# First block's attention: value products of two heads emitted in turn, and the low parts of the keys kept on both halves of the partitions

## The chip, the cores and the metric

The kernel runs on one core of one Trainium2 chip. The metric is the time on the device of one execution, in microseconds (us); a run is repeated, and the median stands. A core has five engines that work beside each other: PE (TensorE, matrix products and, as PEld, the loads of their weights), DVE (VectorE), ACT (ScalarE), POOL (GpSimd) and SP (SyncE, which starts transfers here). PE writes its products to PSUM, from where DVE and ACT fetch them.

## The reference

Two blocks follow each other, each of two layers, on 256 tokens of width 1024 and 256 context tokens. The change lies in the attention of the first block, which is, for one layer:

```python
h  = modulate(rms_norm(x,  norm_mix[l]), sh1, sc1)
hc = modulate(rms_norm(xc, norm_mix[l]), csh1, csc1)
k, v, q, u, f, gt = jnp.split(h @ w_in[l], IN_SPLITS, axis=-1)
kc, vc, qc, uc, fc, gtc = jnp.split(hc @ w_in[l], IN_SPLITS, axis=-1)   # layer 0
q = apply_rope(q.reshape(B, T, N_Q_HEADS, HEAD_DIM), cos, sin)
k = apply_rope(k.reshape(B, T, N_KV_HEADS, HEAD_DIM), cos, sin)
o = latent_attention(q, k, v, kc, vc, attn_sink[l])
x = x + g1 * merge_branches(o, u, f, gt, ...)
oc = context_attention(qc, kc, vc, attn_sink[l])                        # layer 0 only
```

There are 8 query heads on 2 key/value heads, of 64 channels each. A latent query sees the 256 latent keys, under a window of 128 to either side, the 256 context keys, and one sink column in the softmax. A context query (layer 0 only) sees the context keys and the sink. `latent_attention` is products q k, mask, softmax, and products of the probabilities p with v. The same layer holds a pooling branch, a Fourier branch, 24 gate tiles and a merge, then a feed-forward part with a convolution. The second block holds stick-breaking attention, an mLSTM, a spatial gating and a feed-forward part that gathers 128 experts for each token. All is computed in float32.

## The kernel before

The whole is one program, and a scheduler sets the order of the instructions on each engine; PE then runs in that order. Activations lie with channels on the 128 partitions and tokens along the free dimension.

Dense products (`fm`, `mm3`, lines 165 to 182) split both operands into a high and a low part and add three products for each block of 128 channels: high by high (L169), low by high (L170), high by low (L171). One such product has 512 columns in layer 0 (latents and context) and 256 in layer 1 (latents only). In the trace such operands are named `b`, `hi` and `lo`, and their PSUM tiles `mm`.

In `layer1` the query tile `ot` (passed on as `qt`) holds, for head m + 4·kv, the high part of the query on the partitions of kv (0 to 63 for kv 0, 64 to 127 for kv 1) and the low part on the other 64. `keys()` (lines 489 to 504) fills `kt` with three slots of 512: slot kv holds the high part of kv's keys on both halves, slot 2 the low part of kv 0's keys on the lower 64 partitions and of kv 1's on the upper 64. `tt` (L117) is a two-tensor operation on DVE. `kt` and the values `vu` appear as `s` in the trace, query tiles as `b`.

In `attention` each head is a generator with three stages:

1. scores: one product of 128 partitions with slot kv (both parts of the query by the high part of the keys), one of 64 with slot 2 (high part of the query by the low part of the keys), for latents one masking product with `k_mask`; then maximum and bias on DVE and the exponential on ACT.
2. the probabilities are transposed in blocks of 128 (L138, a product with the identity `k_sq`) and copied from PSUM (`ptb`, in the trace `t`), by ACT for odd heads, by DVE for even ones.
3. value products: for each block of 128 keys one product of 64 channels into `ob`, an `sm` tile of PSUM in which kv 0 owns partitions 0 to 63 and kv 1 the others. There are four blocks for a latent head, two for a context head. In the trace they are `sm<-t,s 128*64`, two records for a product.

All bank products, scores and values alike, pass through `Bank.mm`, so they carry the line 45. For each m, heads are gone through in the order i = 0, 1, 2, ..., with kv = i mod 2; a step of the loop calls stage 3 of head i-2, stage 2 of head i-1 and stage 1 of head i, and then one of the `fill` functions (a gate tile of 24 dense products, a pooling or a Fourier part). Layer 0 has 32 heads (16 latent, 16 context), layer 1 has 16, all latent. `mod_step` (L264 in layer 0) spreads a product with the modulation weights through the program: four of its products share one bank on different strips of it.

`ptb` and the other 512-wide tiles come from a pool of five buffers (`t2`); the `sm` tiles of PSUM from a pool of four banks.

Of the kernel before, what the change touches and what calls it, by code (L numbers as in the profile page):

```python
# [10 lines left out]
F32 = mybir.dt.float32  # L11
F32R = mybir.dt.float32r
# [4 lines left out]
OP = mybir.AluOpType  # L17
AX = mybir.AxisListType

P = 128  # L20
# [9 lines left out]
HALVES = ((slice(0, 64), 0), (slice(64, 128), 1))  # L30
# [36 lines left out]
class Kernel:  # L67
# [375 lines left out]
    def layer1(self, l, x):  # L443
# [8 lines left out]
        def rope(out, src):  # L452
            raw = self.t2([P, 512])[:, :T]
            self.copy(raw, src)
            rot = self.psum("sm")[:, :T]
            nc.tensor.matmul(rot, rotm, raw, start=True, stop=True)
            a = self.t2([P, 512])[:, :T]
            b = self.t2([P, 512])[:, :T]
            self.tt(a, raw, cosT, OP.mult)
            self.tt(b, rot, sinT, OP.mult)  # L460
            self.tt(out, a, b, OP.add)

        vk = self.s8([P, 2048])
        ff = self.s8([P, 2, 512])
        kt = self.s8([P, 3, 512], F32R)
        vu = vk[:, :1536].rearrange("p (b c) -> p b c", b=4)
        banks = [self.psum("sm") for _ in range(2 if last else 4)]
        for u in range(4):
# [5 lines left out]
            for tb, bank in enumerate(banks):  # L474
                for kk in range(2):
                    k = 2 * u + kk
# [12 lines left out]
        def keys():  # L489
            ps = self.fm(self.unit(d["w_in"][l, 0]), h, 0, KD, 0, 512)  # L490
            k = self.t2([P, 512])
            rope(k[:, :T], ps[:, :T])
            self.copy(k[:, T:], ps[:, T:])
            for r, i in HALVES:
                self.copy(kt[r, i], k[r])
                self.copy(kt[HALVES[1 - i][0], i], k[r])
                self.tt(kt[r, 2], k[r], kt[r, i].bitcast(F32), OP.subtract)
            if last:
                vt = self.t2([P, 512])[:, :T]
                self.copy(vt, self.fm(self.unit(d["w_in"][l, 31]), h, 0, KD, T, 512))  # L500
                ps = self.psum("sm")
                for tb in range(2):
                    self.transpose(ps[:, tb * P:(tb + 1) * P], vt[:, tb * P:(tb + 1) * P])
                self.copy(vu[:, 2:, :P], ps[:, :T].rearrange("p (b c) -> p b c", b=2))

        if not last:
            keys()
# [19 lines left out]
        if last:  # L527
            keys()
# [27 lines left out]
        for m in range(KD):  # L556
            w = self.unit(d["w_br"][l, m])
            acc = None
            for b, src, wk0, nk in ((1, po, 4, 2), (2, fo, 6, 2), (0, o, 0, 4)):
# [3 lines left out]
                if acc is not None:  # L563
                    s = self.t2([P, 512])[:, :n]
# [21 lines left out]
    def attention(self, l, kt, qt, vu, o, n):  # L586

        nc = self.nc  # L590
        nsink = self.sb([P, 8], "ns")
        self.ts(nsink, self.sink[:, l], -1.0, None, OP.mult)
        nq = n // P

        def head(m, i, blk):
            qb, kv = divmod(i, 2)
            lat = qb < 2
            k0, nk = (0, 512) if lat else (T, T)
            nb = nk // P
            if i == 0:  # L600
                blk.update(ob=Bank(self, "sm"), nm=self.sb([P, 8], "c1"), den=self.sb([P, 8], "c1"))
            ob, nm, den = blk["ob"], blk["nm"], blk["den"]
            hh = kv * 4 + m
            r = slice(kv * 64, kv * 64 + 64)
            qs = slice(qb * P, (qb + 1) * P)
            bank = Bank(self, "sm")
            s = bank.t[:, :nk]
            bank.mm(s, qt[:, m + 4 * kv, qs], kt[:, kv, k0:k0 + nk])
            bank.mm(s, qt[r, m + 4 * kv, qs], kt[r, 2, k0:k0 + nk])
            if lat:  # L610
                b = 1 - qb
                bank.mm(s[:, b * P:(b + 1) * P], *((self.le_neg, self.ident16) if qb else (self.ident16, self.le_neg)))
            mx = self.sb([P, 1], "m1")
            nc.vector.tensor_reduce(mx, s, axis=AX.X, op=OP.max)
            self.ts(nm[:, i:i + 1], mx, -0.125, nsink[:, hh:hh + 1], OP.mult, OP.min)
            p = self.t2([P, 512])[:, :nk]
            self.act(p, s, AF.Exp, scale=0.125, bias=nm[:, i:i + 1], accum_out=den[:, i:i + 1])
            yield
            pt = self.psum("sm")
            for b in range(nb):  # L620
                self.transpose(pt[:, b * P:(b + 1) * P], p[:, b * P:(b + 1) * P])
            ptb = self.t2([P, 512])
            self.copy(ptb[:, :nk], pt[:, :nk], "act" if i % 2 else "dve")
            yield
            for b in range(nb):
                ob.mm(ob.t[r, qs], vu[:, k0 // P + b, r], ptb[:, b * P:(b + 1) * P], rows=kv)
            if i < 2 * nq - 1:
                return
            e = self.sb([P, 8], "c1")
            two = lambda a: a[:, :2 * nq].rearrange("p (q v) -> p q v", v=2)  # L630
            self.tt(two(e), self.sink[:, l].rearrange("p (v m) -> p m v", v=2)[:, m, None, :].to_broadcast([P, nq, 2]),
                    two(nm), OP.add)
            e2 = self.sb([P, 8], "c1")
            self.act(e2[:, :2 * nq], e[:, :2 * nq], AF.Exp)
            self.tt(den[:, :2 * nq], den[:, :2 * nq], e2[:, :2 * nq], OP.add)
            rec = self.sb([P, 8], "c1")
            nc.vector.reciprocal(rec[:, :2 * nq], den[:, :2 * nq])
            rw = self.t2([P, 512])[:, :n]
            self.copy(rw.rearrange("p (h e) -> p h e", e=64), rec[:, :2 * nq, None].to_broadcast([P, 2 * nq, 64]),
                      "dve")  # L640
            rt = self.psum("sm")[:, :n]
            for q in range(nq):
                self.transpose(rt[:, q * P:(q + 1) * P], rw[:, q * P:(q + 1) * P])
            rs = self.t2([P, 512])[:, :n]
            self.copy(rs, rt)
            on = self.t2([P, 512])[:, :n]
            self.tt(on, ob.t[:, :n], rs, OP.mult)
            self.split(on, o[0][:, m, :n], o[1][:, m, :n])

        stages = []  # L650
        for m in range(4):
            blk = {}
            for i in range(2 * nq):
                stages.append(head(m, i, blk))
                for st in stages[-3:]:
                    next(st, None)
                yield
        for st in stages[-2:] + stages[-1:]:
            next(st, None)
# [762 lines left out]
```

## Time and profile before

| what | us |
|---|---|
| median of three runs (lowest, highest) | 2964.41 (2963.31, 2968.53) |
| the profiled execution, its whole time | 2967.73 |
| its span in the trace | 2965.9 |
| PE busy | 2606.1 (88%) |
| DVE busy | 1935.2 (65%) |
| ACT busy | 1057.9 (36%) |
| POOL busy | 549.7 (19%) |

The span is cut into stretches by what runs in them. The attention of the first block's layer 0 lies between 126 and 350 us, that of layer 1 between about 869 and 955 us, both among the dense products of the gates. A share of busy time over the span says little of one stretch, so the stretches have their own table. [...] Matmul records overlap in the listing: each lasts longer than the time to the next, so what one product costs is read from start to start.

### The profile page before, as it was taken

What the parts mean: (1) busy time and instruction counts of PE and PEld (TensorE: products, weight loads), DVE (VectorE), ACT (ScalarE), POOL (GpSimd) and SP (SyncE); (2) the same over time, 40 slices, a digit from 0 to 9 for tenths busy, and PEclk for the clock granted to TensorE, in tenths of its full rate; (3) what the DMA queues carried; (4) which work ended last, traced back from release to release, by engine and by line L of the source; (5) the groups of instructions that cost most, each with busy time, mean ns of one, the idle gap of its engine ahead of it and who ended that gap; (6) DMA issues with size and microseconds to landing.
All of it is one profiled execution on the core that took longest, in us unless ns stands there. A gap on an engine that the chain in (4) does not pass through costs nothing.

```text
span 2965.9 us, 33988 instructions
## 1 busy us (share of the span) xinstructions
PE 2606.1 (88%) x11870; PEld 1772.3 (60%) x11870; DVE 1935.2 (65%) x4268; ACT 1057.9 (36%) x2173; POOL 549.7 (19%) x559
## 2 busy tenths in 40 slices
PE   6999999999999999999688887877897889687777
PEld 4666777888888999988344332322786444232222
DVE  4324468998365688667676869554577666975554
ACT  3333334443254465455233323111463332331111
POOL 0000000000000000010433343333112333233332
PEclk9999999999999999999899899999999999889999
DMA  6432134556342445542999999999325999889998
GB/s 245 142 121 89 65 110 167 192 188 189 92 149 93 164 164 198 158 135 83 388 419 418 408 416 411 420 420 420 128 100 189 419 418 419 357 361 420 420 420 358
DMA packets 140569, 776.35 MB, mean 262 GB/s; under 512 B 15728, under 2 KB 18800, under 8 KB 73328
## 3 DMA queue, kind: packets, MB, share of 16 engines
q0 software_dynamic: 73728, 536.90, 43.9%
q1 hardware_dynamic: 66672, 237.28, 23.9%
q8 instruction: 95, 1.56, 0.2%
q14 instruction: 74, 0.61, 0.1%
HBM read 773.08 MB, written 1.05 MB: 261 GB/s over the span
## 4 chain that ended last, share of the span: by engine, by line
PE 31%; DMA 22%; DVE 13%; issue 2%; ACT 2%; POOL 1%; POOLq 0%; ACTq 0%; SPq 0%; DVEq 0%
DMA b<-in_peer_uv_dram,b 19%; PE y L1134 9%; PE mm L169 5%; PE mm L170 5%; PE mm L171 5%; DVE b L1150 4%; DMA raw<-in_peer_wq_dram 3%; PE sm L45 2%; DVE t L117 2%; DVE t L1191 1%; DVE b L1194 1%; PE mm L45 1%; DVE b L1193 1%; DVE lo L134 1%; ACT hi L133 1%
## 5 line engine op out<-in xcount | busy, mean ns | idle before, releaser
L1134 PE MATMUL y<-b,lo 128*128 128x512 f32 x2048 | 985.6, 633 | 269.5 <-ACT lo L129 266.8
L1134 PEld LDWEIGHTS y<-b,lo 128*128 128x128 f32 x2048 | 397.8, 201 | 827.7 <-issue 430.6
L1150 DVE SCALAR_TENSOR_TENSOR b<-xt,b 128x1024 f32<-128x1024 f32 x512 | 620.0, 1221 | 270.4 <-DMA b<-in_peer_uv_dram,b 269.5
L1146 POOL DMA_INDIRECT b<-in_peer_uv_dram,b x512 | 499.1, 975 | 852.9 <-DMA b<-in_peer_uv_dram,b 338.5
L134 DVE TENSOR_TENSOR lo<-raw,hi 128x1024 fp32r<-128x1024 f32 (+1 forms) x339 | 406.1, 1199 | 282.3 <-ACT hi L133 247.8
L133 ACT ACTIVATE hi<-raw 128x1024 fp32r<-128x1024 f32 (+1 forms) x339 | 351.7, 1039 | 551.3 <-PE mm L170 289.9
L169 PE MATMUL mm<-b,hi 128*128 128x512 f32 (+1 forms) x1512 | 530.8, 353 | 4.3 <-ACT b L133 1.7
L171 PE MATMUL mm<-b,lo 128*128 128x512 f32 (+1 forms) x1512 | 525.7, 348 | 0.0
L170 PE MATMUL mm<-b,hi 128*128 128x512 f32 (+1 forms) x1512 | 525.5, 348 | 0.0
L319 POOL TENSOR_TENSOR c<-c,k_mhalf 128x4 f32<-128x4 f32 (+2 forms) x39 | 45.0, 1155 | 1534.7 <-DVE c L123 1533.9
L169 PEld LDWEIGHTS mm<-b,hi 128*128 128x128 f32 x1512 | 285.9, 189 | 57.4 <-issue 6.9
L170 PEld LDWEIGHTS mm<-b,hi 128*128 128x128 f32 x1512 | 286.5, 190 | 37.9 <-issue 2.6
L171 PEld LDWEIGHTS mm<-b,lo 128*128 128x128 f32 x1512 | 286.6, 190 | 36.5 <-issue 1.4
L129 ACT ACTIVATE b<-b 128x2 f32<-128x2 f32 (+2 forms) x280 | 61.9, 221 | 670.0 <-DVE b L1150 662.4
L169 PE MATMUL mm<-s,hi 128*128 128x256 f32 (+2 forms) x976 | 284.6, 295 | 7.4 <-ACT s L133 5.2
L171 PE MATMUL mm<-s,lo 128*128 128x256 f32 (+2 forms) x976 | 281.7, 292 | 0.0
L170 PE MATMUL mm<-s,hi 128*128 128x256 f32 (+2 forms) x976 | 279.6, 288 | 0.8 <-DVE s L134 0.6
L129 ACT ACTIVATE lo<-k_sq,b 128x128 f32<-128x128 f32 x512 | 178.6, 394 | 181.0 <-DVE b L117 172.9
L169 PEld LDWEIGHTS mm<-s,hi 128*128 128x128 f32 (+1 forms) x976 | 187.1, 193 | 17.5 <-ACT s L133 7.3
L170 PEld LDWEIGHTS mm<-s,hi 128*128 128x128 f32 (+1 forms) x976 | 187.6, 193 | 5.5 <-issue 2.4
L171 PEld LDWEIGHTS mm<-s,lo 128*128 128x128 f32 (+1 forms) x976 | 187.0, 193 | 3.6 <-issue 2.6
L117 DVE TENSOR_TENSOR b<-b 128x2 f32<-128x2 f32 (+3 forms) x272 | 45.9, 170 | 102.0 <-ACT b L129 101.9
(241 smaller groups left out, 2404.9 us busy)
## 6 DMA issues: line engine op xcount, KB each, us to landing
raw<-in_w_in_dram SPq DMA_DIRECT2D x97, 512.0 KB, 3.3
raw<-in_w_up_dram SPq DMA_DIRECT2D x88, 512.0 KB, 3.3
raw<-in_w_mod_dram SPq DMA_DIRECT2D x80, 512.0 KB, 3.3
raw<-in_w_out_dram SPq DMA_DIRECT2D x32, 512.0 KB, 3.2
raw<-in_w_down_dram SPq DMA_DIRECT2D x32, 512.0 KB, 3.5
raw<-in_peer_wq_dram SPq DMA_DIRECT2D x32, 512.0 KB, 8.5
b<-in_w_mod_dram SPq DMA_DIRECT2D x8, 1024.0 KB, 13.8
raw<-in_w_br_dram SPq DMA_DIRECT2D x16, 512.0 KB, 3.3
```

Source lines behind the costliest of these rows:

```text
L45: ins = k.nc.tensor.matmul(out, lhsT, rhs, start=first is None, stop=True, skip_group_check=True)
L117: self.nc.vector.tensor_tensor(out, a, b, op=op)
L129: self.nc.scalar.activation(out, in_, fn, **kw)
L133: return (self.nc.scalar.activation(hi, x, AF.Copy), self.nc.vector.tensor_tensor(lo, x, hi.bitcast(F32), op=OP.subtract))
L134: self.nc.vector.tensor_tensor(lo, x, hi.bitcast(F32), op=OP.subtract))
L169: mm(ps, sh, mh, start=first, stop=False)
L170: mm(ps, sh, ml, start=False, stop=False)
L171: mm(ps, sl, mh, start=False, stop=last)
L319: self.nc.gpsimd.tensor_tensor(r[:, :n], v[:, :n], self.mhalf[:, :n], op=OP.pow)
L1134: nc.tensor.matmul(bank["y"][c], dg[:, i], rows[:, i, D + 512 * c:D + 512 * (c + 1)], start=h == 0 and k + i == 0, stop=h == 7 and k + i = ...
L1146: nc.gpsimd.indirect_dma_start(out=rows[:, i], out_offset=None, in_=table[:, :], in_offset=bass.IndirectOffsetOnAxis(ap=part["idx"][:, tb, ...
L1150: self.nc.vector.scalar_tensor_tensor(rows[:, i, :D], bank["x"], 1.0, rows[:, i, :D], op0=OP.mult, op1=OP.mult, accum_out=part["act"][:, t ...
```

## The change

Two things are done. The tile of the keys gets a fourth slot: slot 2 + kv now holds the low part of kv's keys on both halves of the partitions, which takes two more subtractions of 64x512 in each layer. The second score product then runs over all 128 partitions, with the whole query tile as in the first (so it also adds the low part of the query by the low part of the keys). And the even head of a pair (kv 0) no longer emits its value products in its third stage: it leaves its transposed probabilities in `blk["even"]`, and the odd head emits the products of both, one of kv 0 and one of kv 1 in turn for each block of keys.

```diff
@@ layer1
-        kt = self.s8([P, 3, 512], F32R)
+        kt = self.s8([P, 4, 512], F32R)
...
             for r, i in HALVES:
                 self.copy(kt[r, i], k[r])
                 self.copy(kt[HALVES[1 - i][0], i], k[r])
-                self.tt(kt[r, 2], k[r], kt[r, i].bitcast(F32), OP.subtract)
+                for half in (r, HALVES[1 - i][0]):
+                    self.tt(kt[half, 2 + i], k[r], kt[r, i].bitcast(F32), OP.subtract)
@@ attention
             bank.mm(s, qt[:, m + 4 * kv, qs], kt[:, kv, k0:k0 + nk])
-            bank.mm(s, qt[r, m + 4 * kv, qs], kt[r, 2, k0:k0 + nk])
+            bank.mm(s, qt[:, m + 4 * kv, qs], kt[:, 2 + kv, k0:k0 + nk])
...
             self.copy(ptb[:, :nk], pt[:, :nk], "act" if i % 2 else "dve")
             yield
+            if kv == 0:
+                blk["even"] = ptb
+                return
             for b in range(nb):
-                ob.mm(ob.t[r, qs], vu[:, k0 // P + b, r], ptb[:, b * P:(b + 1) * P], rows=kv)
+                for rv, pv, v in ((HALVES[0][0], blk["even"], 0), (r, ptb, 1)):
+                    ob.mm(ob.t[rv, qs], vu[:, k0 // P + b, rv], pv[:, b * P:(b + 1) * P], rows=v)
```

The order on SP and POOL is the same before and after. On PE, in layer 0's second step, before the change: the value products of head 0 (tile `t_155_807`) and those of head 1 (`t_167_875`) stand a step apart. The earlier of the two places:

```order
L138 MATMUL sm_855<-k_sq_66,t_164_853 128x128 x4
L45 MATMUL sm_753<-t_155_807,s_27_130 64x128 x4
L138 MATMUL sm_870<-k_sq_66,t_158_816 128x128 x4
L45 MATMUL sm_877<-s_29_132,b_88_475 128x512 x2
L45 LDWEIGHTS k_mask_72
```

and the later one, one step on, behind a product of the modulation weights (L264):

```order
L171 MATMUL mm_892<-b_25_128,lo_889 128x512
L264 MATMUL ax_917<-raw_919,k_sc_82 2x512 x2
L45 MATMUL sm_753<-t_167_875,s_27_130 64x128 x4
L138 MATMUL sm_928<-k_sq_66,t_170_884 128x128 x4
L45 MATMUL sm_935<-s_29_132,b_88_475 128x512 x2
L45 LDWEIGHTS k_mask_72
```

After the change the later place on PE holds both heads' value products (the numbers of the tiles shift by two), and the earlier one none:

```order
L264 MATMUL ax_915<-raw_917,k_sc_82 2x512 x2
L45 MATMUL sm_755<-t_155_809,s_27_130 64x128
L45 MATMUL sm_755<-t_167_873,s_27_130 64x128
L45 MATMUL sm_755<-t_155_809,s_27_130 64x128
L45 MATMUL sm_755<-t_167_873,s_27_130 64x128
L45 MATMUL sm_755<-t_155_809,s_27_130 64x128
L45 MATMUL sm_755<-t_167_873,s_27_130 64x128
L45 MATMUL sm_755<-t_155_809,s_27_130 64x128
L45 MATMUL sm_755<-t_167_873,s_27_130 64x128
L138 MATMUL sm_930<-k_sq_66,t_170_882 128x128 x4
```

The eight products alternate between the two heads, so between the two halves of the PSUM tile `sm_755`. The rows of a score pair read the same in both orders (`128x512 x2`): the change from 64 to 128 partitions does not show there.

On PE in layer 1, before the change, between a head's transposes (`sm_6673`, copied to `t_1257_6678`) and its value products stand the next scores, the mask and six dense products:

```order
L138 MATMUL sm_6673<-k_sq_66,t_1251_6635 128x128 x4
L45 MATMUL sm_6680<-s_1102_5883,b_1120_5982 128x512 x2
L45 LDWEIGHTS k_mask_72
L45 MATMUL sm_6680<-k_mask_72 128x128
L169 MATMUL mm_6747<-b_1098_5879,hi_6743 128x256
L170 MATMUL mm_6747<-b_1099_5880,hi_6743 128x256
L171 MATMUL mm_6747<-b_1098_5879,lo_6744 128x256
L169 MATMUL mm_6747<-b_1098_5879,hi_6743 128x256
L170 MATMUL mm_6747<-b_1099_5880,hi_6743 128x256
L171 MATMUL mm_6747<-b_1098_5879,lo_6744 128x256
L45 MATMUL sm_6555<-t_1257_6678,s_1100_5881 64x128 x4
```

After the change, at the same transposes of layer 1 on PE:

```order
L138 MATMUL sm_6673<-k_sq_66,t_1251_6639 128x128 x4
L45 MATMUL sm_6680<-s_1102_5885,b_1120_5984 128x512 x2
L45 LDWEIGHTS k_mask_72
L45 MATMUL sm_6680<-k_mask_72 128x128
L45 MATMUL sm_6555<-t_1248_6630,s_1100_5883 64x128
L45 MATMUL sm_6555<-t_1257_6678,s_1100_5883 64x128
L45 MATMUL sm_6555<-t_1248_6630,s_1100_5883 64x128
L45 MATMUL sm_6555<-t_1257_6678,s_1100_5883 64x128
```

The second value product, the first that reads `t_1257_6678`, now has only the scores, the mask and one value product between itself and the transposes; the dense products have gone elsewhere.

In ten of the 24 groups the scheduler draws the first product of the even head forward, between dense products. One such place on PE in layer 1, after the change:

```order
L170 MATMUL mm_6573<-b_1099_5882,hi_6569 128x256
L171 MATMUL mm_6573<-b_1098_5881,lo_6570 128x256
L45 MATMUL sm_6351<-t_1220_6505,s_1100_5883 64x128
L169 MATMUL mm_6647<-b_1098_5881,hi_6643 128x256
L170 MATMUL mm_6647<-b_1099_5882,hi_6643 128x256
```

The other seven of that group stand together some twenty rows further on, and begin and end with a product of the odd head.

## Rows read from the trace of the kernel before

**Rows 1.** The page: busy time, share of span, instructions of each engine.

```profile
PE 2606.1 (88%) x11870; PEld 1772.3 (60%) x11870; DVE 1935.2 (65%) x4268; ACT 1057.9 (36%) x2173; POOL 549.7 (19%) x559
```

**Rows 2.** Busy time by stretch: window, sum; PE, PEld, DVE, ACT, POOL; clock, DMA, GB/s.

```profile
300.00:348.00 48.00, 48.00 (x237) 36.14 (x236) 16.32 (x31) 16.31 (x33) 0.00 (x0) 1.00 0.20 66
348.00:354.00 6.00, 4.33 (x15) 3.19 (x14) 3.09 (x5) 1.59 (x3) 0.00 (x0) 0.73 0.00 0
...
877.00:955.00 78.00, 77.96 (x563) 65.87 (x563) 40.46 (x78) 37.14 (x77) 0.00 (x0) 1.00 0.29 95
```

**Rows 3.** PE's groups by form: tiles, shape, count | busy us, mean ns | idle.

```profile
L45 PE MATMUL sm<-t,s 128*64 128x128 f32 x320 | 45.2, 280 | 0.0
...
L45 PE MATMUL sm<-s,b 64*128 64x512 f32 x32 | 15.8, 495 | 0.0
```

**Rows 4.** Timeline of PE in layer 0: start us, duration us, operation, count.

```profile
202.43 1.03 PE L264 MATMUL ax<-raw,k_sc 128*2 128x512 f32 x4
203.38 1.09 PE L45 MATMUL sm<-t,s 128*64 128x128 f32 x8
204.40 0.66 PE L138 MATMUL sm<-k_sq,t 128*128 128x128 f32 x4
204.81 0.90 PE L45 MATMUL sm<-s,b 128*128 128x512 f32 x2
...
206.00 0.39 PE L170 MATMUL mm<-b,hi 128*128 128x512 f32 x1
206.22 0.40 PE L171 MATMUL mm<-b,lo 128*128 128x512 f32 x1
```

**Rows 5.** The weight loads beside it, in brackets the idle time before.

```profile
205.22 0.18 PEld L45 LDWEIGHTS sm<-s,b 64*128 64x128 f32 x1 [0.24 <-issue]
```

**Rows 6.** Timeline of PE at a context head of layer 0.

```profile
213.73 0.67 PE L45 MATMUL sm<-s,b 128*128 128x256 f32 x2
...
214.66 0.40 PE L170 MATMUL mm<-b,hi 128*128 128x512 f32 x1
```

**Rows 7.** Timeline of PE in the second block's spatial gating (L1059).

```profile
1357.97 0.66 PE L1059 MATMUL sm<-b,b 128*64 128x128 f32 x8
1358.56 0.49 PE L1061 MATMUL sm<-b 128*128 128x128 f32 x2
```

**Rows 8.** Timeline of all engines at the end of layer 0's attention.

```profile
346.11 0.38 PE L138 MATMUL sm<-k_sq,t 128*128 128x128 f32 x2
...
346.58 0.38 ACT L112 ACTIVATE t<-sm 128x256 f32<-128x256 f32 x1 [1.04 <-PE sm L138]
...
347.11 0.65 PE L45 MATMUL sm<-t,s 128*64 128x128 f32 x4
...
347.70 0.66 PE L138 MATMUL sm<-k_sq,t 128*128 128x128 f32 x4
...
348.45 0.60 ACT L112 ACTIVATE t<-sm 128x512 f32<-128x512 f32 x1 [1.49 <-PE sm L138]
...
350.49 0.98 PE L169 MATMUL mm<-b,hi 128*128 128x512 f32 x2 [1.67 <-ACT b L133]
```

**Rows 9.** Timeline of PE at a group of value products in layer 1.

```profile
899.17 0.28 PE L170 MATMUL mm<-b,hi 128*128 128x256 f32 x1
899.29 0.28 PE L171 MATMUL mm<-b,lo 128*128 128x256 f32 x1
899.50 1.09 PE L45 MATMUL sm<-t,s 128*64 128x128 f32 x8
900.52 0.39 PE L169 MATMUL mm<-b,hi 128*128 128x256 f32 x1
900.74 0.28 PE L170 MATMUL mm<-b,hi 128*128 128x256 f32 x1
```

**Rows 10.** Timeline of DVE behind layer 1's keys.

```profile
868.82 1.40 DVE L117 TENSOR_TENSOR s<-t,s 64x512 fp32r<-64x512 f32 x2
871.73 0.69 DVE L614 TENSOR_REDUCE m<-sm 128x1 f32<-128x512 f32 x1 [1.51 <-PE sm L45]
```

## The prediction

> **What bounds the kernel now.** I read the page first, for which engine carries the time: PE is busy for 88% of the span [rows 1]. That is a mean over stages, so I next read the table of busy time by stretch over the two stretches in which the first block's attention runs, 126 to 348 us (layer 0) and 877 to 955 us (layer 1). PE is busy for all of 300 to 348 and for 77.96 of the 78 us of layer 1, at a granted clock of 1.00, while DVE and ACT are busy for a third to a half and the DMA share is 0.20 to 0.29 [rows 2]; the stretches from 126 to 300 read alike. The list of waits names none for PE in either stretch. There every microsecond taken off PE's stream moves all that follows, until another engine becomes late. Behind both stretches the dense products go on, so I pass savings on to the end one to one.
>
> Then I read PE's own rows, because "busy" hides how well the array is fed. The value products have 320 records, two for each of 160 products [rows 3]. In the timeline a group of eight begins at 203.38 and the next operation at 204.40: 1.02 us [rows 4]. A record streams 128 columns twice, 0.109 us at this clock, so eight stream in 0.87; the other 0.15 is the last one draining and the next weights coming late. A group of four takes 347.11 to 347.70, 0.59 [rows 8]. And the spatial stage has eight records of exactly this shape, four on either half of the array's columns, in turn: 1357.97 to 1358.56, 0.59 for eight, as long as four on one half [rows 7]. Products on different column halves run at the same time.
>
> **The change, part by part.**
>
> *Scores.* There are 48 pairs, 32 of 512 keys [rows 3] and the 16 context heads of layer 0 with 256. From the first record of a 512 pair to the second dense product behind it: 204.81 to 206.00, 1.19 us [rows 4]. The streams in that stretch are two of 512 columns and one dense product of 512, 0.227 each (206.00 to 206.22 is such a product), plus the mask's one pass of 128 columns, 0.055: 0.74. What is left, 0.45, lies where the array goes from 128 rows to 64 and back: the weight load of the 64-row product stood idle 0.24 before it began and the product started with it, at 205.22 [rows 5]. After the change both products have 128 rows and the second load can lie under the first stream. Then it is 0.08 before the first stream (an estimate: transposes begun at 204.40 still stream), 2 x 0.227, the mask and its load 0.11, the dense 0.227: 0.87. Saved 0.32, times 32 is 10.1 us. A pair of 256 goes from 213.73 to 214.66, 0.93 [rows 6], against 0.08 + 2 x 0.114 + 0.227 = 0.535: saved 0.40, times 16 is 6.3. Together **16.3**. The multiply-adds added (64 more rows) cost no columns. Bounds: 8 (only one of the two switches goes) to 19 (the whole remainder).
>
> *Value products.* Before: 32 groups of eight records at 1.02 and 16 of four at 0.59, 42.1 us. Where the neighbour is an ordinary 128-column product the group costs also its entry, since 899.29 to 899.50 is 0.21 where records of that kind are 0.12 apart, and its exit, since 900.52 to 900.74 is 0.22: 0.19 in all [rows 9]. In the order 33 of the 48 groups have such neighbours: 6.3. Sum 48.4. After: 16 groups of sixteen records and 8 of eight. Eight cost 0.59 by the spatial row, sixteen 0.59 + 4 x 0.109 = 1.03: 16 x 1.03 + 8 x 0.59 = 21.2. With 14 ordinary neighbours, 2.7. But the order shows that in 10 of the 24 groups one product is drawn forward, away from the others. Such a product runs alone: two records 0.22, drain 0.15, entry and exit 0.19, so 0.55 each, 5.5 us. Sum 29.4; saved **19.0**. Bounds: 12 (the ten splits cost double, each of the 160 rounds 0.01 more) to 24 (the splits cost only their columns).
>
> *What it costs.* The pair of L264 products in front of a group runs its four records in 0.95, both halves at once [rows 4]; the changed order parts one such pair, and it pays about that again: 0.95. The value products of the odd head stand closer behind its transposes. Before, from a head's transposes to its value products, 346.11 to 347.11, dense products filled the time, and ACT's copy lay between, from 346.58 for 0.38 [rows 8]. In the changed order of layer 1 shown above only scores, mask and one value product stand between. With four blocks the last transpose starts 0.33 after the first, the copy begins 0.36 later and takes 0.60 for 512 columns [rows 8], and 0.15 passes behind it: 1.44, where PE has the transposes, the pair, the mask and that one product to do, some 1.1. So 0.35 of waiting. I count five of 24 pairs as close as that: 1.7. All 24 would be 8.4; none, 0. Of the two subtractions added per layer (64x512, 0.70 each), those of layer 1 stand at 868.82, and DVE's next work there had idled 1.51 us [rows 10]; they cost nothing, and at most 2.8 us if that cover were gone in both layers. SP and POOL have the same order; no DMA is moved past another. Loss **2.6**, bounds 0 to 12.
>
> [...] In the spatial row eight records leave in 0.59, so pairs start within 0.109 [rows 7]. [...]
>
> **The sum.** 16.3 + 19.0 - 2.6 = 32.7. The profiled execution took 2967.73 us, 1.8 more than its span and 3.3 above the median of the runs, 2964.41. So 2935.0 for an execution like the profiled one, and for the median 2964.4 - 32.7, about **2932 us**.
>
> **The rivals.**
>
> *The halves do not overlap here.* If the weight load of the second half must wait for the product that runs on the first, the rounds cost two records each, 160 x 0.109 = 17.4 us more. Only the scores stay: 2932 + 17.4, about 2949. Against it stand the spatial rows, whose records have all 128 rows and differ in the column half alone [rows 7]. For it: there nothing is accumulated from block to block, here four blocks add into one bank. [...]
>
> *The second score product stays as dear.* If the 0.24 of [rows 5] is not the change of rows but the load waiting for the first product itself, 16.3 falls away: about 2948. Against it: the dense products before and behind, all of 128 rows, follow each other without that gap.
>
> *Slower: PE waits for the bunched heads and its clock falls.* Two heads' value products now hang on the later head's copy. [...] Against it: the estimate gives 0.35 for the closest pairs, and 19 have more work between.
>
> *The change does not do what it says.* The scheduler could part the halves again, so that they run alone. The order shows that it parts one product off in ten groups, which leaves two products without a partner there, so 140 of 160 keep theirs; were all parted, the time would be the first rival's.
>
> **How the numbers follow.** Forecast 0.80, halves not overlapping 0.06, score pair unchanged 0.05, both failing 0.03 (nothing left but the losses: 2964.4 + 2, within 0.2%), slower 0.06 of which 0.02 ends within 0.2%. 0.2%, 5.9 us, is about what a measurement of this kernel can tell from no change. So faster 0.91, within 0.05, slower 0.04. The bounds of the terms would reach 43 and 8 if all went one way together; about half of that to either side, and the runs' own spread of 2963.31 to 2968.53, gives 2921 to 2945 for the forecast, with some 0.70 of its 0.80. To hold 8 in 10 the range must reach to the two rivals at 2948 and 2949: 2921 to 2950.
>
> **What would show it.** After the change a group of sixteen value records should last 1.0 to 1.1 us to the next operation, and one of eight 0.6; if 1.9 and 1.0, the halves do not overlap. The second score record should start about 0.23 behind the first's stream and the first dense product about 0.87 - 0.23 = 0.64 after the first record; if 0.87, the row switch was not the cost. PE's waits in both attention stretches should stay under 3 us with the clock at 1.00; more, or a clock under 0.95, speaks for the slower case. The dense products should be untouched, and layer 0's attention some 21 us and layer 1's some 11 us shorter. A gain in these that does not arrive at the end would make the one-to-one passing wrong.

## The result and the profile after

| what | before | after |
|---|---|---|
| median of the runs, us | 2966.47 (2963.31 to 2970.86, four runs) | 2936.31 (2934.13 to 2938.20, four runs) |
| the profiled execution, us | 2967.73 | 2938.20 |
| its span, us | 2965.9 | 2936.4 |
| PE busy, us | 2606.1 | 2565.1 |

The ratio of after to before is 0.9896, with a 95% interval of 0.9885 to 0.9908: 30 us, or 1.04%, faster. The prediction was 2932 us in a range of 2921 to 2950, and 32.7 us saved.

The list of PE's groups by form (tiles, shape, count | busy us, mean ns | idle) shows what has become of [rows 3]:

```profile
L45 PE MATMUL sm<-t,s 128*64 128x128 f32 x320 | 27.1, 282 | 0.0
L45 PE MATMUL sm<-s,b 128*128 128x512 f32 x64 | 22.8, 438 | 0.0
L45 PE MATMUL sm<-s,b 128*128 128x256 f32 x32 | 7.7, 323 | 0.0
```

There are still 320 value records, of 282 ns each, but together they keep PE busy for 27.1 us in place of 45.2: they lie over one another. The form with 64 rows is gone; all 64 + 32 score records have 128.

In PE's timeline of after, at the place in layer 0 that the order shows (start us, duration us, operation, count), the rows that answer to [rows 4], which are from a later place of the same shape:

```profile
131.51 1.03 PE L264 MATMUL ax<-raw,k_sc 128*2 128x512 f32 x4
132.47 1.09 PE L45 MATMUL sm<-t,s 128*64 128x128 f32 x16
133.50 0.66 PE L138 MATMUL sm<-k_sq,t 128*128 128x128 f32 x4
133.91 0.71 PE L45 MATMUL sm<-s,b 128*128 128x512 f32 x2
134.46 0.23 PE L45 MATMUL sm<-k_mask 128*128 128x128 bf16 x1
134.50 0.47 PE L169 MATMUL mm<-b,hi 128*128 128x512 f32 x1
134.81 0.39 PE L170 MATMUL mm<-b,hi 128*128 128x512 f32 x1
```

Sixteen value records take 132.47 to 133.50, 1.03 us, where eight took 1.02. The score pair reaches its second dense product after 0.90 (133.91 to 134.81), in the kernel before after 1.19. The weight loads of the pair are now one row of two, with no idle time ahead of the second:

```profile
133.88 0.30 PEld L45 LDWEIGHTS sm<-s,b 128*128 128x128 f32 x2
134.46 0.10 PEld L45 LDWEIGHTS <-k_mask 128*128 128x128 bf16 x1 [0.27 <-issue]
```

A context head of layer 0, answering to [rows 6], takes 141.53 to 142.08, 0.55 in place of 0.93:

```profile
141.53 0.48 PE L45 MATMUL sm<-s,b 128*128 128x256 f32 x2
141.85 0.39 PE L169 MATMUL mm<-b,hi 128*128 128x512 f32 x1
142.08 0.40 PE L170 MATMUL mm<-b,hi 128*128 128x512 f32 x1
```

How far the program has come behind both attentions is read from one product of layer 1's Fourier branch, 960.72 us in before and 927.99 in after (the line number moves with the text):

```profile
960.72 1.03 PE L688 MATMUL sm<-b,s 128*128 128x256 f32 x4
```

```profile
927.99 1.03 PE L694 MATMUL sm<-b,s 128*128 128x256 f32 x4
```

That is 32.7 us, the predicted sum. Some 21.3 of them are there already where layer 1's keys are split (868.82 in [rows 10], 847.53 in the row shown further down), so 11.4 come from layer 1; 21 and 11 were forecast. At the end of this pair of executions 29.5 are left (2965.9 - 2936.4).

### The profile page after: what moved, and what is told of

Read it like the earlier page. It is cut to its first block, busy times and chain, and to the rows that moved or that the text cites. A ratio compares the mean times of both kernels' runs of the same rounds, so it can differ in the third digit from the quotient of the medians.

```text
span 2936.4 us, 33987 instructions
## 1 busy us (share of the span) xinstructions
PE 2565.1 (87%) x11870; PEld 1750.2 (60%) x11870; DVE 1937.0 (66%) x4272; ACT 1057.4 (36%) x2173; POOL 551.1 (19%) x559
## 4 chain that ended last, share of the span: by engine, by line
PE 29%; DMA 23%; DVE 14%; ACT 2%; issue 2%; POOL 1%; POOLq 0%; ACTq 0%; DVEq 0%; SPq 0%
DMA b<-in_peer_uv_dram,b 20%; PE y L1140 8%; PE mm L169 5%; PE mm L170 5%; PE mm L171 5%; DVE b L1156 5%; DMA raw<-in_peer_wq_dram 4%; DVE t L117 2%; PE sm L45 1%; DVE t L1197 1%; DVE b L1200 1%; PE mm L45 1%; DVE b L1199 1%; ACT hi L133 1%; DVE lo L134 1%
```

## The experiments

My theory: two separate savings on a PE that has no slack, the switch of rows in the score pair and the overlap of the two column halves, less what the new order loses. The main rivals: one of the two does nothing, or the gain comes from having half as many groups and not from emitting them in turn.

**Each part alone.** The first kernel has this edit of the kernel before and nothing else:

```diff
-        kt = self.s8([P, 3, 512], F32R)
+        kt = self.s8([P, 4, 512], F32R)
...
-                self.tt(kt[r, 2], k[r], kt[r, i].bitcast(F32), OP.subtract)
+                for half in (r, HALVES[1 - i][0]):
+                    self.tt(kt[half, 2 + i], k[r], kt[r, i].bitcast(F32), OP.subtract)
...
-            bank.mm(s, qt[r, m + 4 * kv, qs], kt[r, 2, k0:k0 + nk])
+            bank.mm(s, qt[:, m + 4 * kv, qs], kt[:, 2 + kv, k0:k0 + nk])
```

> The kernel before with the fourth slot of the keys and the second score product over 128 partitions; the value products stay as before, each head's alone. Theory (the two parts are separate, the score pair saves what the trace of the change shows, 0.29 us for each of 32 pairs of 512 keys and 0.38 for each of 16 pairs of 256): 15.3 us less than the kernel before, ratio 0.9948. Rival (the score saving hangs on the new order of heads, which this kernel does not have): no difference. Rival (the two further subtractions delay the first scores): 1 to 3 us less saved than 15.3.

The second has the other half of the change, in the kernel before:

```diff
+            if kv == 0:
+                blk["even"] = ptb
+                return
             for b in range(nb):
-                ob.mm(ob.t[r, qs], vu[:, k0 // P + b, r], ptb[:, b * P:(b + 1) * P], rows=kv)
+                for rv, pv, v in ((HALVES[0][0], blk["even"], 0), (r, ptb, 1)):
+                    ob.mm(ob.t[rv, qs], vu[:, k0 // P + b, rv], pv[:, b * P:(b + 1) * P], rows=v)
```

> The changed kernel with the keys and the second score product as before (three slots, 64 partitions); only the value products are emitted in pairs, in turn. Theory: value groups of 1.03 and 0.59 us in place of 1.02 and 0.59 twice, ten groups parted, one L264 pair parted: 17 us less than the kernel before, ratio 0.9943; this and the kernel with the scores alone add up to the whole change (32). Rival (the parts share a gain, such as a wait that either removes): the sum of the two is 5 us or more away from 32.

Beside runs of the kernel before with a median of 2967.50, the scores alone took 2952.32 (ratio 0.9947, 0.9934 to 0.9961), 15.2 us less, and the values alone 2949.37 (0.9936, 0.9923 to 0.9950), 18.1 less. Both parts work by themselves: 15.3 and 17 were expected, and 33.3 together is not apart from the 30 to 32 of the whole change. The two rivals in which a saving hangs on the other part fall.

**Is it the alternation?** One edit of the changed kernel:

```diff
-            for b in range(nb):
-                for rv, pv, v in ((HALVES[0][0], blk["even"], 0), (r, ptb, 1)):
+            for rv, pv, v in ((HALVES[0][0], blk["even"], 0), (r, ptb, 1)):
+                for b in range(nb):
```

> The changed kernel, but a pair's value products are emitted one head after the other: four of the lower half, then four of the upper, where the change has them in turn. Theory (the gain is the two column halves running at the same time): each large group takes 2 x 0.87 + 0.15 = 1.89 in place of 1.03 and each small one 1.02 in place of 0.59, 16 x 0.86 + 8 x 0.43 = 17.2 us slower than the changed kernel, less up to 2.4 for the one record at each seam that can overlap, and less up to 4 because a product drawn forward now loses no partner: 11 to 17 us slower than the change, ratio to the kernel before 0.993 to 0.995. Rival (the gain is that 48 groups became 24, with fewer entries and exits): as the change, ratio 0.9896.

It took 2941.83 (0.9910, 0.9896 to 0.9923): 25.7 us less than before, some 4 to 7 slower than the change (30.2 to 32.4 less than before in its own runs), and so neither what I expected nor what the rival did. PE's timeline of this kernel shows why. A large group, and then a small one:

```profile
132.04 1.58 PE L45 MATMUL sm<-t,s 128*64 128x128 f32 x16
133.55 0.66 PE L138 MATMUL sm<-k_sq,t 128*128 128x128 f32 x4
```

```profile
164.02 0.67 PE L45 MATMUL sm<-t,s 128*64 128x128 f32 x8
164.62 0.44 PE L138 MATMUL sm<-k_sq,t 128*128 128x128 f32 x2
```

Four products of one half and then four of the other take 1.51, neither 1.89 nor 1.03. In the single records of the trace the first half's fifth of eight starts at 132.525 and the second half's first at 132.531: the second half does not wait for the seam but starts when four records of the first are left, the fifth among them (which record is whose is read from their spacing). With two and two products the second half starts at once, and the small group takes 0.60, as in turn (0.59). In one group whose first product is drawn forward, so that six records of the first half are left, the second half's first record (890.001) starts with the third of the six (889.995): again four are left, so it is this count that matters and not a wait for the odd head's copy. So the halves overlap also when they don't alternate, as far as four records reach. Part of this kernel's loss has another cause: in six of its 24 pairs the scheduler sets the two heads' products apart, with other work between, and each head then runs alone:

```profile
258.53 1.09 PE L45 MATMUL sm<-t,s 128*64 128x128 f32 x8
259.55 1.99 PE L700 MATMUL sm<-b,t 128*128 128x256 f32 x8
...
264.38 1.09 PE L45 MATMUL sm<-t,s 128*64 128x128 f32 x8
265.40 0.50 PE L170 MATMUL mm<-b,hi 128*128 128x512 f32 x1
```

That is twice 1.02 in place of 1.03 (three pairs), and twice 0.58 in place of 0.59 (three small ones). From the groups that stay together I formed a new theory, that PE runs records of one half beside up to four pending ones of the other, and tested it with two products of the odd head, two of the even head, and again. This is an edit of the held kernel of the next experiment:

```diff
-            for b in range(nb):
-                for rv, pv, v in ((r, ptb, 1), (HALVES[0][0], blk["even"], 0)):
+            for b, v in [(b0 + d, v) for b0 in range(0, nb, 2) for v in (1, 0) for d in range(2)]:
+                for rv, pv in ((HALVES[v][0], ptb if v else blk["even"]),):
```

> As the kernel that holds each group together (odd head first, nothing drawn forward), but two products of the odd head, then two of the even head, and again two and two, where that kernel has them in turn. In the trace of the kernel with four and four, the second half's first record began together with the first half's fifth of eight, so records of one half run beside up to four pending records of the other. Theory (PE looks four records ahead): two products are four records, so the halves still overlap fully; a large group takes 1.03 us and the time is that of the held kernel in turn, ratio 0.9879. Rival (only neighbours overlap, and the four-and-four trace showed something else): a large group takes 1.4 us or more, 16 x 0.4 = 6 us slower, ratio 0.990 or above.

It took 2933.62 (0.9883, 0.9867 to 0.9900), not apart from the held kernel in turn below, and its large group, 132.61 to 133.69, lasts 1.08, near the 1.03 of the theory, in place of the 1.51 of four and four:

```profile
132.61 1.15 PE L45 MATMUL sm<-t,s 128*64 128x128 f32 x16
133.69 0.55 PE L138 MATMUL sm<-k_sq,t 128*128 128x128 f32 x3
```

The theory of four records agrees with both; where the limit comes from is not shown.

**The products drawn forward.** In each pair of the changed kernel the odd head now comes first, and every product of the even head is ordered behind its first one:

```diff
+            odd = None
             for b in range(nb):
-                for rv, pv, v in ((HALVES[0][0], blk["even"], 0), (r, ptb, 1)):
-                    ob.mm(ob.t[rv, qs], vu[:, k0 // P + b, rv], pv[:, b * P:(b + 1) * P], rows=v)
+                for rv, pv, v in ((r, ptb, 1), (HALVES[0][0], blk["even"], 0)):
+                    ins = ob.mm(ob.t[rv, qs], vu[:, k0 // P + b, rv], pv[:, b * P:(b + 1) * P], rows=v)
+                    if odd is None:
+                        odd = ins.ins.name
+                    elif v == 0:
+                        self.tc.add_manual_dep(
+                            ins.ins, odd,
+                            mybir.DependencyInfo(mybir.DependencyClass.NoSync, mybir.DependencyReason.DATA),
+                            reason="pairs")
```

> The changed kernel, but in each pair the odd head's product comes first and every product of the even head is held behind the odd head's first one in the order, so that none is drawn forward. Theory (a product drawn forward costs its 0.36 us alone plus an entry of 0.1 to 0.2, while the group it left is no shorter): nine or ten times 0.5, so 4 to 5 us faster than the changed kernel, less up to 1.5 for waits on the odd head's copy; ratio to the kernel before 0.9880 to 0.9887. Rival (the scheduler drew it forward because PE would stand still, and waits take its place): as the change, 0.9896, with waits of PE at the value products of 3 us or more in the trace.

In PE's timeline of the changed kernel a parted group stands so, its first product alone and then fourteen records:

```profile
860.71 0.23 PE L45 MATMUL sm<-k_mask 128*128 128x128 bf16 x1
860.87 0.43 PE L45 MATMUL sm<-t,s 128*64 128x128 f32 x2
861.24 0.39 PE L170 MATMUL mm<-b,hi 128*128 128x256 f32 x1
...
861.90 1.09 PE L45 MATMUL sm<-t,s 128*64 128x128 f32 x14
862.92 0.39 PE L171 MATMUL mm<-b,lo 128*128 128x256 f32 x1
```

The single product takes 0.36 to the next operation, and the fourteen records 1.02, no less than sixteen. In the held kernel the same group is whole:

```profile
859.40 1.09 PE L45 MATMUL sm<-t,s 128*64 128x128 f32 x16
860.42 0.39 PE L170 MATMUL mm<-b,hi 128*128 128x256 f32 x1
```

It took 2932.07 (0.9879, 0.9864 to 0.9894), at the fast end of what the theory gave. Beside the changed kernel on one chip:

> The held kernel (odd head first, nothing drawn forward) once more, on one chip with the changed kernel. Theory (the nine products drawn forward and alone cost 0.36 plus an entry each): 4 to 5 us less than the changed kernel beside it. Rival (the difference between the two earlier calls was that of chips): within 2 us of it.

> The changed kernel beside the held one, for the difference of the two: 4 to 5 us more than the held kernel by the theory, within 2 us by the rival. Behind its first wait on ACT's b of L129 the clock may read 0.83 or 1.00: the two profiles of this program so far show one each.

Here the held kernel took 2931.78 (2928.03 to 2939.80; 0.9884, 0.9869 to 0.9899) and the changed one 2935.79 (2932.41 to 2937.66; 0.9888, 0.9873 to 0.9903). The medians differ by 4.0 us, as those of the earlier runs do (2936.31 and 2932.07, not taken side by side), but the runs and the intervals overlap, and the two ratios, 0.9884 and 0.9888, are only 1.2 us apart. The traces show that no lone product is drawn forward any more (one group still stands in two parts, of four and twelve records) and that no waits came in its place: every whole group takes 0.59 or 1.02 to 1.03. Added up over all groups, from the first record to the next operation, the value products take 24.7 us in the changed kernel and 21.3 in both executions of the held one, which is 3.5 less before the entries. So the gain on PE is shown; the 4 us at the end stay a likely figure. The held kernel and its form with two and two are the fastest of the kernels here that compute all of the reference. The changed kernel once more, beside the next two:

> The changed kernel once more, beside the kernels of this call. Theory: 30 to 32 us less than the kernel before, ratio 0.9890 to 0.9900.

It took 2935.88 (0.9885, 0.9869 to 0.9902), 32.4 less than the 2968.28 of the kernel before, a little more than expected.

**What the second score product still costs.** It is left out of the changed kernel altogether:

```diff
-            bank.mm(s, qt[:, m + 4 * kv, qs], kt[:, 2 + kv, k0:k0 + nk])
```

> The changed kernel without the second score product: the queries by the low part of the keys is left out, in all 48 heads. Theory (over 128 partitions that product costs only its stream): 32 x 0.227 + 16 x 0.114 = 9.1 us less than the changed kernel, ratio to the kernel before 0.9865. Rival (a switch or a late weight load is still in it, 0.1 to 0.28 us each): 14 to 22 us less than the changed kernel.

It took 2928.21 (0.9862, 0.9846 to 0.9879), 7.7 less than the changed kernel beside it, nearer to 9.1 than to 14. In its rows, from the score to the next operation, a pair of 512 goes from 0.554 to 0.320 and one of 256 from 0.320 to 0.203: 32 x 0.234 + 16 x 0.117 = 9.4. So over 128 rows the product of 512 columns costs 0.234, where a dense product of 512 takes some 0.227: its stream and next to nothing else.

**Is it the switch of rows?** In the kernel before, both products now have 64 rows:

```diff
-            bank.mm(s, qt[:, m + 4 * kv, qs], kt[:, kv, k0:k0 + nk])
+            bank.mm(s, qt[r, m + 4 * kv, qs], kt[r, kv, k0:k0 + nk])
```

> The kernel before with the first score product over 64 partitions too: the low part of the queries by the high part of the keys is left out, so both products of a pair have 64 rows and the switch from 128 to 64 rows lies between the transposes and the pair instead of inside it. Theory (what costs is each switch between 128 and 64 rows, and there are two per pair either way): as the kernel before, within 2 us, ratio 0.9993 to 1.0007. Rival (each product of 64 rows loads its weights late): 48 x 0.24 = 11 us slower, ratio 1.004. Rival (only a switch between the two products of one bank costs): about 8 to 9 us faster, ratio 0.997.

It took 2968.34 beside 2968.28 (0.9999, 0.9989 to 1.0009). Its timeline:

```profile
204.88 0.66 PE L138 MATMUL sm<-k_sq,t 128*128 128x128 f32 x4
205.46 0.73 PE L45 MATMUL sm<-s,b 64*128 64x512 f32 x2
206.12 0.23 PE L45 MATMUL sm<-k_mask 128*128 128x128 bf16 x1
206.16 0.47 PE L169 MATMUL mm<-b,hi 128*128 128x512 f32 x1
206.47 0.39 PE L170 MATMUL mm<-b,hi 128*128 128x512 f32 x1
```

From the transposes to the pair it is now 0.58, where [rows 4] has 0.41; from the pair to the second dense product 1.01, there 1.19. What the pair lost, its entry gained, and from 204.88 to 206.47 it is 1.59, before 1.60, after the change 1.31. Twice as many products of 64 rows cost nothing; the two switches cost the same wherever they stand. The late weight load as a price of each product falls, and so does a cost of the two products sharing a bank.

## Why the prediction was right, point by point

*PE as the bound, one to one.* This held. PE's list of waits in after has one entry for both attention stretches, where layer 0's ends:

```profile
PE mm L169 <- ACT b L133: 1.4, 1, 1.4
```

32.7 us were gained at the product behind both attentions, and 30.2 to 32.4 at the end by the medians of three comparisons. That 32.7 meets the forecast to the tenth is luck in part: before and after each have one fall of the granted clock, the share of PE's full speed, in the 100 us behind layer 0's attention (0.73 over 348 to 354, 0.83 over 417.2 to 427.2; last section), and two further executions of the changed kernel, without a fall there, reach the product at 927.47 and 927.26, so 33.2 and 33.5 earlier than before does. In all three executions of the changed kernel 3.0 to 3.4 us are given back behind that product, against the one kept execution of before. The kernel with both products of 64 rows, whose time is that of before, loses 1.4 us against the same execution over the same way, so about that much belongs to that one execution. The rest I leave open; it is within the spread of the runs, and that a little less than one to one arrives is not ruled out.

*Scores, 16.3 predicted.* By the rows 0.29 x 32 + 0.38 x 16 = 15.4, by the kernel with that part alone 15.2. A pair of 512 after the change is 0.03 dearer than I had set it: from its start to the mask it takes 0.554 (0.534 set), from the mask to the second dense product 0.35 (0.34). The reason given, the switch between 128 and 64 rows, is the one the experiment bears out.

*Value products, 19.0 predicted.* The large group takes 1.025 in the mean of nine undisturbed ones (1.03 predicted), the small one 0.588 (0.59), a single product 0.363 plus its entry (0.55 in all). From 32.7 gained, with 15.3 of the scores and 1.2 of the losses below, 18.6 are left to them. The records give nearly the same: all groups, from the first record to the next operation, add up to 41.8 us before and 24.7 after, 0.27 of it the wait below, so 17.4 less. The entries and exits were set too high on both sides, which cancels: 6.3 before and 4.6 after (2.7 and the ten times 0.19 of the single products) charge a group with an ordinary neighbour on one side for both. In the traces 48 sides before and 33 after have such a neighbour, at some 0.095 each 4.6 and 3.1. The ten parted places are nine groups, one of them parted twice, and not ten groups. Reading the price of a new pattern from a stage elsewhere in the trace with the same shape, [rows 7], gave it to a hundredth of a microsecond. Sixteen records take 1.03, with the 0.15 in it that the prediction set beside eight streams of 0.109, so some 55 ns each. In before's group at 203.38 the second record starts 0.160 behind the first (203.385, 203.545), the others 0.109 apart, and the next operation 0.203 behind the last (204.200, 204.403), together with its weight load, ahead of which PEld had idled 0.17. So about 0.05 of the 0.15 lies at the group's start and 0.09 at its end, where the weights come late; that a record drains there was an estimate of mine and is not shown. Nor is it shown that a record streams its columns twice: it rests on 0.109 being near twice the 0.057 of 128 columns of a dense product (0.227 / 4).

*The first rival, halves that do not overlap.* It fell: sixteen records that add four blocks into one bank take 1.03, where eight on one half took 1.02, so the accumulation does not matter here. In the rows of PEld above the two loads of a score pair last from 133.88 to 134.18 without a gap, while the pair's first product, of the same 128 rows, runs from 133.91. So the second load does not wait for that product to end; why it need not is not shown.

*The losses, 2.6 predicted.* The parted L264 pair costs what was said: each half alone takes 0.95, the pair had taken 0.96. Of the five close pairs only one waited:

```profile
878.58 0.23 PE L45 MATMUL sm<-k_mask 128*128 128x128 bf16 x1
878.74 1.37 PE L45 MATMUL sm<-t,s 128*64 128x128 f32 x16
880.04 0.38 PE L169 MATMUL mm<-b,hi 128*128 128x256 f32 x1
```

This is the place shown in the order. The group takes 1.30 in place of 1.025, so 0.27 of waiting (0.35 predicted), and the list of waits does not name it. The other four did not wait, so 1.7 was too much by 1.4; my count took distances in the order for distances in time. The lowered scores and these smaller losses nearly cancel, which is why the sum came out so close: that is luck.

*The bounds.* Three of them do not follow from their own words. The whole remainder of the scores would be 22 us (0.45 x 32 + 0.475 x 16) and not 19; value products whose splits cost their columns, 10 x 0.22, would save 22 and not 24; and 2921, the lower end of the range, is the whole way to a saving of 43 and not half of it. None of this moved the forecast.

*The subtractions.* They cost nothing, but the cover was thin. DVE in layer 1, answering to [rows 10]:

```profile
847.53 2.80 DVE L117 TENSOR_TENSOR s<-t,s 64x512 fp32r<-64x512 f32 x4
850.25 0.68 DVE L616 TENSOR_REDUCE m<-sm 128x1 f32<-128x512 f32 x1
```

The maximum now follows without the 1.51 of idle time: of that 1.40 is used up.

*The slower case.* No bunching of waits appeared in the attentions and their clock is 1.00 (126 to 328 and 856 to 922); the fall some 90 us behind layer 0's is told below.

## What to carry to other kernels

Where PE is busy throughout, look at how its records start: two products with 64 output channels each, on different halves of the array's columns, ran here in the time of one as long as they stood within about four records of each other (1.03 us for sixteen records in turn, 1.02 for eight on one half, 1.51 for four and four products). A product with half the rows between full ones was dearer here than the full one (1.19 us against 0.90 for the pair of 512 up to the second dense product); where the operand can be padded, keep one form. When a pairing is made, see in the order whether the scheduler draws a lone product forward, and hold it with an ordering dependence.

## What the runs showed of the hardware

*The reach of four records* across the column halves, with 1.51 us for four and four products, 1.08 for two and two, 1.03 in turn. Across the halves PE did not start records in the order of the program: with four and four, the second half's first record, the ninth in that order, starts at 132.531, and the first half's sixth, seventh and eighth only at 132.634, 132.743 and 132.852.

*The price of changing between 128 and 64 rows:* 0.28 us for a pair of 512 (0.835 to 0.554, from its start to the next operation) and the same for a pair of 256 (0.604 to 0.320), for the way there and back.

*The clock behind a wait is not a matter of the kernel alone.* In before the wait of 1.67 us that ends layer 0's attention was followed by a clock of 0.73 [rows 2, 8]; in after the wait there is 1.43, and the stretch 327 to 333 shows 1.00. Some 90 us later, behind a wait of 1.5 us on ACT in both, it is the other way round. Busy time by stretch there (window, sum; PE, PEld, DVE, ACT, POOL; clock, DMA share, GB/s), of before, of after, and of the other execution of the same changed program:

```profile
440.00:450.00 10.00, 8.83 (x33) 4.46 (x34) 10.00 (x27) 5.57 (x13) 0.00 (x0) 1.00 0.59 207
```

```profile
417.20:427.20 10.00, 8.86 (x30) 4.28 (x30) 10.00 (x27) 5.60 (x13) 0.00 (x0) 0.83 0.58 206
```

```profile
418.30:428.30 10.00, 8.80 (x33) 4.45 (x34) 10.00 (x27) 5.54 (x13) 0.00 (x0) 1.00 0.55 206
```

In after the microseconds from 419 to 421 of this stretch read 0.50, and the whole of it lost 0.17 x 10 = 1.7 us; in before those from 351 to 354 read 0.50, and 348 to 354 lost 0.27 x 6 = 1.6. The same program as after lost nothing there in its other execution, nor in the third one, beside the held kernel (1.00 over 418.3 to 428.3 and over 418 to 428). The wait behind layer 0's attention is no better a sign: it lasts 1.67 us in seven of the twelve kept executions, and the clock falls behind it in two of them; in the held kernel's second execution the stretch 325 to 331 shows 1.00. Behind the later wait, of about 1.5 us in all twelve, it falls in four. So some 1.6 to 1.7 us come and go behind such a wait from one execution to the next, and a gain of that size read from one pair of traces is none.
